# Fewer instructions for the S5 tables, the norms and the reciprocal roots of a two-layer hybrid kernel, and a start that scales one block

## The chip, the cores and the metric

One NeuronCore of one Trainium2 chip runs the whole program. The metric is the time of one execution in device microseconds (us), as the median of several runs; lower is better.

## The reference

Two layers work on 1024 latent and 256 context tokens of width 1024. In each layer the tokens are normalized and modulated, multiplied by an input matrix, sent through four mixers of width 256 (a gated delta rule, S5, SSD, attention), multiplied by an output matrix, normalized and modulated again, and sent through a feed-forward net of width 4096.

```python
def _rms(x, g):
    y = xf * lax.rsqrt(jnp.mean(jnp.square(xf), axis=-1, keepdims=True) + EPS)
def _modulate(h, g, shift, scale):
    return _rms(h, g) * (1.0 + scale) + shift
def s5_mixer(...):
    lam_bar = jnp.exp(lam * jnp.exp(log_step)[..., None])
    b_bar = ((lam_bar - 1.0) / lam)[..., None] * lax.complex(b_re, b_im)
```

The shift and scale come from `cond @ w_mod + b_mod`. S5 is a linear recurrence with complex rates `lam_bar`: 2 directions, 16 groups, 64 states, 16 channels per group.

## The kernel before, in words

**Blocks.** Tokens lie in three blocks: 0 (256 context tokens), 1 and 2 (512 latent tokens each). They are handled in the order 2, 0, 1. Every large product is made of three single-pass products, high by high, high by low and low by high, so each weight and each activation is split into `w_hi`, `w_lo`, `a_hi`, `a_lo`. ACT casts `w_hi`, POOL or DVE subtracts to get `w_lo`; `norm` makes `a_hi` on ACT and `a_lo` on POOL or DVE.

**Streams.** The program is written as generators ("streams"). `Streams.run` always steps the one whose virtual time is least; a step of work adds its cost, divided by the stream's number in `SHARE`, to that time. This sets the order in which instructions are handed over and, with it, their precedence. It is not the final order in an engine: the trace shows small steps of a later S5 setup between steps of an earlier product, so a scheduler fills each engine with what it takes to be ready. On the chip each engine then runs its own queue in order.

**Start** (`main`). `hT` is loaded in three DMAs. The stream "tables" runs `s5_tables(0)`. Beside it `main` spawns `norm_scale` for all three blocks (squares on ACT, a sum tree on DVE, a column of ones on PE, `rsqrt` on DVE, a transpose on PE to spread the root over partitions, `n_acc`) and `mod_pe`, which loads 16 blocks of `w_mod` in four DMAs and computes shift and scale (`md`, `gs`) in four groups on PE. When all are done `norm_next` spawns, block after block, `norm` (`n_x` = h times the root on DVE, then `a_hi`, then `a_lo`), and `w_in1` multiplies by the first part of the input matrix; its first six cells take two weight blocks over blocks 2, 0, 1 in turn.

**S5 tables.** `s5_tables` goes through 2 directions x 2 halves. `s5_setup` loads rates, steps and B, C of 8 groups, and computes the exponential of the step (`exp_acc`, 15 DVE instructions), phases (`s5_reduce`, 5 DVE instructions), sines and cosines (`s5_trig`), 17 complex powers per group (nine for E1 and eight, the same in the other order, for Wo), and the scaled B. Then four calls of `s5_products` each make for two groups `E1` (`5_t_hh`), `ow` (in the tile `5_t_k`), two PE products and two transposes of them, and the two factors `co`, `si`; all goes into a tile `5_fc`, which is stored to DRAM. Every one of these tiles has one buffer. For layer 1 the same stream runs beside the feed-forward net of layer 0 (`extra`), after layer 1's modulation.

**What waits for the tables.** The stream `beside` (gates, gated delta rule, and S5 if the main stream has not taken it) starts when the tables and the norms of the layer are done. `main` goes on with `w_in1`, `w_in2`, SSD, attention, S5, the output matrix, the feed-forward net.

**Reciprocal root.** `rsqrt` starts from a bit trick and makes four Newton steps of four DVE instructions each. It is called for every norm and in the mixers.

Of the kernel before, what the change touches and what calls it, by code (L numbers as in the profile page):

```python
# [36 lines left out]
S5_TB = (("pre", (8, 17)), ("pim", (8, 17)), ("rho", (8,)), ("tsn", (2, 8, 16)), ("tcs", (2, 8, 16)),  # L37
# [21 lines left out]
def const_table():  # L59
    p = np.arange(128)  # L60
    i = np.arange(128)
    c = {}
    c["ident"] = (p[:, None] == i[None]).astype(np.float32)
    c["triU"] = (p[:, None] <= i[None]).astype(np.float32)
    c["triL"] = (p[:, None] >= i[None]).astype(np.float32)
    c["ones"] = np.ones((128, 128), np.float32)
    sel = np.zeros((128, 16), np.float32)
    for k in range(2):
        for pr in range(2):
            for d in range(2):  # L70
# [20 lines left out]
    ex = np.zeros((2, 17), np.float32)  # L91
    ex[0, :9], ex[1, :9] = np.arange(9), 8 - np.arange(9)
    ex[0, 9:], ex[1, 9:] = 7 - np.arange(8), np.arange(8)
    c["ex"] = np.tile(ex.reshape(1, 34), (128, 1))
# [19 lines left out]
class Engine:  # L114
# [14 lines left out]
    def cost(self, op, aps):  # L129
# [4 lines left out]
        if self.name == "tensor":  # L134
# [12 lines left out]
SHARE = {"start": 1.4006, "norm": 7.9949, "mod": 0.7917, "tables": 3.0591, "conv": 0.1388, "ffn": 5.4917,  # L147
# [3 lines left out]
         "ssd_1": 0.8561, "s5_1": 3.3729, "chain": 1.0205, "heads": 0.4024, "scan": 1.0954, "factors": 2.0471}  # L151
# [58 lines left out]
class Core:  # L210
# [57 lines left out]
    def rsqrt(self, pool, out, x, eps, scale, post=1.0):  # L268
# [10 lines left out]
        for k in range(4):  # L279
            nc.vector.tensor_tensor(u, y, y, op=OP.mult)  # L280
            nc.vector.tensor_tensor(u, u, a, op=OP.mult)
            nc.vector.tensor_scalar(u, u, -0.5, 1.5, op0=OP.mult, op1=OP.add)
            o = out if (k == 3 and post == 1.0) else y
            nc.vector.tensor_tensor(o, y, u, op=OP.mult)
# [920 lines left out]
    def s5_tables(self, l, bk, side="left"):  # L1205

        with self.pool("s5w", side) as ws:
            for d in range(2):
                for q in range(2):
                    tb = s5_views(self.t(ws, [128, TBW], F32, "5_tb"), S5_TB)  # L1210
                    yield from self.s5_setup(l, d, q, tb, ws)
                    for n in range(4):
                        fc = self.t(ws, [128, FCW], F32, "5_fc")
                        yield from self.s5_products(l, ws, tb, d, slice(2 * n, 2 * n + 2), s5_views(fc, S5_FC), 4 * q + n, bk)
                        self.nc.sync.dma_start(self.s5d[l][:, 4 * q + n, d], fc)

    def s5_products(self, l, ws, tb, d, x, fc, n, bk):
# [3 lines left out]
        pre, pim, bb, cc, sb2 = [tb[k] for k in ("pre", "pim", "bb", "cc", "sb2")]  # L1221
        E1 = self.t(ws, [128, 2, 9, 16], F32, "5_t_hh")
# [31 lines left out]
        for dst, p0, p1, op in ((fc["co"], (ca, cb), (sa, sb), OP.subtract), (fc["si"], (sa, cb), (ca, sb), OP.add)):  # L1254
# [10 lines left out]
            yield  # L1265

# [54 lines left out]
    def s5_setup(self, l, d, q, tb, ws):  # L1321
        nc, A, c = self.nc, self.A, self.c
        NG = 8
        g0 = 16 * d + 8 * q
        gs = slice(g0, g0 + 8)
        self.mark("5_setup")
        prm = self.t(ws, [128, 3, NG], F32, "5_prm", bufs=1)
        nc.sync.dma_start(prm[:, 0:2], A["s5_a"][l][:, :, gs])
        src = A["s5_ls"][l]
        nc.sync.dma_start(prm[:, 2], bass.AP(tensor=src.tensor, offset=src.offset + g0, ap=[[0, 128], [1, NG]]))  # L1330
# [12 lines left out]
        ex = bc(c["ex"][:, 17 * d:17 * d + 17], 1, NG)
# [4 lines left out]
        mag = self.t(ws, [128, NG, 17], F32, "5_t_b", bufs=1)  # L1348
        nc.gpsimd.tensor_tensor(mag, ex, bc(xd, 2, 17), op=OP.mult)
# [5 lines left out]
        rho = tb["rho"]  # L1355
        nc.vector.tensor_scalar(rho, xd, 8.0, None, op0=OP.mult)
        self.exp_acc(ws, rho, rho, "5_ea")

        ph = self.t(ws, [128, 2, NG], F32, "5_ph", bufs=1)
        t8 = self.t(ws, [128, NG], F32, "5_t8", bufs=1)  # L1360
        nc.vector.tensor_scalar(t8, thr, 8.0, None, op0=OP.mult)
        self.s5_reduce(ws, ph[:, 0], t8, None, "5_q")
        nc.vector.tensor_scalar(t8, ph[:, 0], 16.0, None, op0=OP.mult)
        self.s5_reduce(ws, ph[:, 1], t8, None, "5_q")
        yield
# [3 lines left out]
                                ph.rearrange("p a n -> p (a n)"), bc(c["i16"], 1, 2 * NG), "5_t")  # L1369
# [4 lines left out]
        den = self.t(ws, [128, NG], F32, "5_den", bufs=1)  # L1374
# [9 lines left out]
        nc.vector.tensor_tensor(den, are, are, op=OP.mult)  # L1384
        nc.vector.tensor_tensor(w1, aim, aim, op=OP.mult)
        nc.vector.tensor_tensor(den, den, w1, op=OP.add)
        nc.vector.reciprocal(den, den)
# [245 lines left out]
    def norm(self, wk, h, l, i, cs, hi, lo, rb):  # L1633
# [189 lines left out]
    def main(self, out):  # L1823
# [61 lines left out]
        with self.pool("ms") as pm:  # L1885
# [5 lines left out]
            yield [self.norm_scale(pn, h[i], "g", i, rb) for i in blocks] + [self.mod_pe(0, range(16), 4, 4, pm, ("mm", "mm"))]  # L1891
# [9 lines left out]
        for i in blocks:  # L1901
            norm_next(i, 0, 0, rb[i])
# [217 lines left out]
```

## Time and profile before

| what | value |
|---|---|
| median of 3 runs | 4328.35 us (4321.64 to 4334.05) |
| profiled execution, its own time | 4310.99 us |
| its span | 4309.2 us |
| mean granted TensorE clock | 0.931 |
| PE, DVE, ACT, POOL busy | 3817.7, 2716.2, 1259.1, 1455.5 us |

The profiled execution is 17.4 us below the median of the runs. Busy times are unions over an engine's instructions. A DVE instruction that waits for something inside its execution counts as busy. TensorE's clock is given as a share of full speed.

### The profile page before, as it was taken

To read this page: it belongs to the slowest core of one execution; us is meant where nothing else is said; L and a number is where in the kernel's file an instruction comes from. 1 tells how busy PE (TensorE), PEld (TensorE's weight loads), DVE (VectorE), ACT (ScalarE), POOL (GpSimd) and SP (SyncE) were. 2 spreads that over 40 slices of the span, in tenths; PEclk is the share of its full clock that TensorE was granted. 3 is DMA by queue.
4 is the path that set the end of the run, shared out by engine and by line. 5 is a ranking of instruction groups with operands and counts; after the bars stand their busy time and mean duration, and the time that the engine had idled before them with its cause. 6 is when DMAs were issued, how large, how long until landed. Compare 5 with 4: busy or idle time off the path is not lost.

```text
span 4309.2 us, 61386 instructions
## 1 busy us (share of the span) xinstructions
PE 3817.7 (89%) x23280; PEld 3058.1 (71%) x23280; DVE 2716.2 (63%) x6419; ACT 1259.1 (29%) x2015; POOL 1455.5 (34%) x1664
## 2 busy tenths in 40 slices
PE   5789897789978899999999798997959988999999
PEld 2567776667656688887788677775846676888887
DVE  7966567775644799997775645567765536444443
ACT  3324434333312411121222343244322323222121
POOL 3532533454451211133332224435435433222121
PEclk7899998789999999999999899998969999999999
DMA  5347520100345033311111243342041231111111
GB/s 184 125 159 221 194 98 32 45 2 5 74 123 176 30 98 98 103 60 55 50 62 62 81 136 100 106 144 76 14 106 52 58 135 32 57 40 59 40 59 59
DMA packets 170872, 367.29 MB, mean 85 GB/s; under 512 B 46160, under 2 KB 88400, under 8 KB 166864
## 3 DMA queue, kind: packets, MB, share of 16 engines
q1 hardware_dynamic: 170576, 363.37, 26.2%
q8 instruction: 183, 3.00, 0.3%
q14 instruction: 113, 0.93, 0.1%
HBM read 277.42 MB, written 85.89 MB: 84 GB/s over the span
## 4 chain that ended last, share of the span: by engine, by line
PE 46%; DVE 15%; POOL 3%; DMA 2%; ACT 2%; issue 2%; SPq 0%; DVEq 0%; ACTq 0%; POOLq 0%
PE mm L125 38%; PE m L125 3%; DVE mod_acc L125 3%; PE g L125 2%; PE c L125 2%; DVE h L125 2%; DVE n_x L125 1%; PE x L125 1%; DVE s_ca L125 1%; POOL a_lo L125 1%; POOL g_pr L125 1%; DVE g_scr L125 1%; DVE rsq_u L125 1%; SPq L125 0%; DVE f_r L125 0%
## 5 line engine op out<-in xcount | busy, mean ns | idle before, releaser
L125 PE MATMUL mm<-a_hi,w_hi 128*128 128x512 f32 (+1 forms) x2576 | 978.2, 381 | 45.5 <-ACT st L125 28.6
L125 PE MATMUL mm<-a_lo,w_hi 128*128 128x512 f32 (+1 forms) x2576 | 971.4, 378 | 38.0 <-POOL a_lo L125 18.5
L125 PE MATMUL mm<-a_hi,w_lo 128*128 128x512 f32 (+1 forms) x2576 | 965.8, 375 | 2.4 <-DVE w_lo L125 2.4
L125 POOL TENSOR_TENSOR w_lo<-w_raw,w_hi 128x1024 fp32r<-128x1024 f32 x189 | 465.0, 2469 | 1270.9 <-ACT w_hi L125 1268.9
L125 DVE SCALAR_TENSOR_TENSOR h<-mm,md,h 128x512 f32<-128x512 f32 (+1 forms) x680 | 467.4, 693 | 250.7 <-PE mm L125 246.9
L125 PEld LDWEIGHTS mm<-a_hi,w_hi 128*128 128x128 f32 x2576 | 499.1, 194 | 141.9 <-ACT st L125 32.6
L125 PEld LDWEIGHTS mm<-a_lo,w_hi 128*128 128x128 f32 x2576 | 500.4, 194 | 131.0 <-POOL a_lo L125 30.5
L125 PEld LDWEIGHTS mm<-a_hi,w_lo 128*128 128x128 f32 x2576 | 499.3, 194 | 83.9 <-DVE w_lo L125 2.9
L125 PE MATMUL mm<-f_rh,w_hi 128*128 128x512 f32 (+1 forms) x1280 | 478.3, 374 | 27.8 <-DVE f_r L125 13.7
L125 PE MATMUL mm<-f_rl,w_hi 128*128 128x512 f32 (+1 forms) x1280 | 473.6, 370 | 0.0
L125 PE MATMUL mm<-f_rh,w_lo 128*128 128x512 f32 (+1 forms) x1280 | 473.1, 370 | 0.0
L125 ACT CAST w_hi<-w_raw 128x1024 fp32r<-128x1024 f32 x234 | 242.2, 1048 | 735.5 <-PE mm L125 600.5
L125 DVE SCALAR_TENSOR_TENSOR f_r<-mm,f_r 128x512 f32<-128x512 f32 (+1 forms) x160 | 101.5, 634 | 360.1 <-ACT f_rh L125 359.4
L125 PEld LDWEIGHTS mm<-f_rh,w_hi 128*128 128x128 f32 x1280 | 243.7, 190 | 72.0 <-DVE h L125 16.5
L125 PEld LDWEIGHTS mm<-f_rh,w_lo 128*128 128x128 f32 x1280 | 243.1, 190 | 40.5
L125 PEld LDWEIGHTS mm<-f_rl,w_hi 128*128 128x128 f32 x1280 | 243.5, 190 | 39.1
L125 ACT ACTIVATE f_r<-mm 128x512 f32<-128x512 f32 (+1 forms) x160 | 88.1, 551 | 547.7 <-PE mm L125 474.0
L125 DVE SCALAR_TENSOR_TENSOR mod_acc<-mod_w,cond,mod_acc 128x128 f32<-128x128 f32 x672 | 240.4, 404 | 1.4
L125 POOL TENSOR_TENSOR m_sum<-m_sum,m_p 128x512 f32<-128x512 f32 x128 | 164.1, 1282 | 124.0 <-ACT m_p L125 117.9
L125 DVE SCALAR_TENSOR_TENSOR s_ca<-s_cx,s_prm,s_ca 128x255 f32<-128x255 f32 (+2 forms) x240 | 148.7, 644 | 24.4 <-ACT s_ca L125 22.1
L125 POOL TENSOR_TENSOR a_lo<-n_x,a_hi 128x512 fp32r<-128x512 f32 (+1 forms) x66 | 77.8, 1188 | 154.4 <-DVE n_x L125 139.5
L125 DVE TENSOR_TENSOR f_rl<-f_r,f_rh 128x512 fp32r<-128x512 f32 (+1 forms) x160 | 116.1, 726 | 2.0
(493 smaller groups left out, 6629.0 us busy)
## 6 DMA issues: line engine op xcount, KB each, us to landing
w_raw<-in_w_ff SPq DMA_DIRECT2D x128, 512.0 KB, 3.6
w_raw<-in_w_in SPq DMA_DIRECT2D x90, 512.0 KB, 3.9
mod_w<-in_w_mod SPq DMA_DIRECT2D x80, 512.0 KB, 3.7
pd<-st SPq DMA_DIRECT2D x80, 257.0 KB, 2.3
s5d<-5_fc SPq DMA_DIRECT2D x32, 577.0 KB, 2.8
5_fc<-s5d SPq DMA_DIRECT2D x16, 1154.0 KB, 6.3
g_cx<-pd SPq DMA_DIRECT2D x18, 643.0 KB, 4.9
h<-in_hT SPq DMA_DIRECT2D x4, 2048.0 KB, 9.9
```

What stands on the lines that cost most here:

```text
L125: return f(*args, **kw)
```

## The change

1. `s5_small` does the one-number-per-group work (step, rate, phases, `rho`, the reciprocal of |lambda|^2) for all 32 groups at once, once per layer. `s5_setup` takes slices of it.
2. Nine powers per group instead of 17; Wo reads the same nine in reverse.
3. In `s5_products` the PE part, its copies and the E1 and rho copies go behind the `co`/`si` part; `ow` has a tile of its own, `5_t_o`; the rho copy moves from DVE to ACT.
4. `rsqrt` makes three Newton steps of three instructions instead of four of four.
5. `norm` multiplies h by scale and root in one instruction, `n_x` has three buffers, and the low part is one DVE instruction for odd k, ACT and POOL for even k.
6. At the start only `norm_scale` of block 2 runs beside the modulation; blocks 0 and 1 are scaled by their norm streams.
7. Seven numbers in `SHARE` differ.

```diff
-SHARE = {"start": 1.4006, "norm": 7.9949, "mod": 0.7917, "tables": 3.0591, ..., "ffn": 5.4917,
+SHARE = {"start": 2.8429, "norm": 7.0304, "mod": 0.7934, "tables": 2.7961, ..., "ffn": 6.1066,
-... "mla_1": 1.3799, ... "s5_1": 3.3729, ... "scan": 1.0954
+... "mla_1": 1.4932, ... "s5_1": 5.5532, ... "scan": 1.078
...
-        for k in range(4):
-            nc.vector.tensor_tensor(u, y, y, op=OP.mult)
+        for k in range(3):
+            nc.vector.scalar_tensor_tensor(u, y, -0.5, y, op0=OP.mult, op1=OP.mult)
             nc.vector.tensor_tensor(u, u, a, op=OP.mult)
-            nc.vector.tensor_scalar(u, u, -0.5, 1.5, op0=OP.mult, op1=OP.add)
-            nc.vector.tensor_tensor(o, y, u, op=OP.mult)
+            nc.vector.scalar_tensor_tensor(o, u, 1.5, y, op0=OP.add, op1=OP.mult)
...
     def s5_tables(self, l, bk, side="left"):
+            sm = yield from self.s5_small(l, ws)
...
     def s5_products(...):
         E1 = ...
-        nc.scalar.copy(fc["E1"], E1[:, :, 1 - d:9 - d])
-        ow = self.t(ws, [128, 2, 8, 16], F32, "5_t_k")
+        ow = self.t(ws, [128, 2, 8, 16], F32, "5_t_o")
-        nc.vector.tensor_copy(fc["rho"], tb["rho"][:, x])
-        (PE products of E1, transposes of ow, K and Wo copies, store of K)
         (co and si)
+        (PE products of E1, transposes of ow)
+        nc.scalar.copy(fc["E1"], E1[:, :, 1 - d:9 - d])
+        nc.scalar.copy(fc["rho"], tb["rho"][:, x])
+        (K and Wo copies, store of K)
...
     def s5_setup(...):
-        (loads of prm, exp_acc, xd, th, thr, rho, ph, den, 8 groups wide)
+        (slices of s5_small's tiles; one copy phc)
-        mag = self.t(ws, [128, NG, 17], F32, "5_t_b", bufs=1)
+        mag = self.t(ws, [128, NG, 9], F32, "5_t_b", bufs=1)
...
     def norm(...):
-            x = self.t(wk, [128, 512], F32, "n_x", bufs=2)
-            nc.vector.tensor_tensor(x[:, :w], h[:, k], rb[:, :w], op=OP.mult)
-            nc.scalar.activation(hi[:, k], x[:, :w], AF.Identity, bias=sh, scale=gs)
+            x = self.t(wk, [128, 512], F32, "n_x", bufs=3)
+            nc.vector.scalar_tensor_tensor(x[:, :w], h[:, k], gs, rb[:, :w], op0=OP.mult, op1=OP.mult)
+            nc.scalar.activation(hi[:, k], x[:, :w], AF.Identity, bias=sh)
             if k % 2:
-                nc.scalar.activation(x[:, :w], x[:, :w], AF.Identity, bias=sh, scale=gs)
+                nc.vector.scalar_tensor_tensor(lo[:, k], x[:, :w], sh, hi[:, k].bitcast(F32), op0=OP.add, op1=OP.subtract)
             else:
-                nc.vector.tensor_scalar(x[:, :w], x[:, :w], gs, sh, op0=OP.mult, op1=OP.add)
-            (nc.vector if k % 4 == 3 else nc.gpsimd).tensor_tensor(lo[:, k], x[:, :w], hi[:, k].bitcast(F32), op=OP.subtract)
+                nc.scalar.activation(x[:, :w], x[:, :w], AF.Identity, bias=sh)
+                nc.gpsimd.tensor_tensor(lo[:, k], x[:, :w], hi[:, k].bitcast(F32), op=OP.subtract)
...
-            yield [self.norm_scale(pn, h[i], "g", i, rb) for i in blocks] + [self.mod_pe(0, range(16), 4, 4, pm, ("mm", "mm"))]
+            yield [self.norm_scale(pn, h[2], "g", 2, rb), self.mod_pe(0, range(16), 4, 4, pm, ("mm", "mm"))]
...
-            norm_next(i, 0, 0, rb[i])
+            norm_next(i, 0, 0, rb.get(i))
```

## Rows read from the trace of the kernel before

**Rows 1.** By stretch: us, busy (count) of PE, PEld, DVE, ACT, POOL, PEclk, DMA share, GB/s

```profile
0.00:66.00 66.00, 25.90 (x114) 10.59 (x114) 43.07 (x214) 17.79 (x25) 14.47 (x26) 0.82 0.68 247
66.00:146.00 80.00, 53.39 (x173) 34.92 (x173) 72.58 (x189) 34.29 (x59) 46.73 (x52) 0.74 0.21 77
146.00:282.00 136.00, 105.25 (x502) 78.56 (x503) 110.54 (x335) 30.46 (x70) 65.63 (x105) 0.91 0.37 133
282.00:480.00 198.00, 191.36 (x1524) 152.91 (x1523) 103.61 (x209) 88.84 (x148) 56.77 (x74) 0.97 0.73 234
...
1866.00:2316.00 450.00, 427.76 (x2201) 356.98 (x2201) 334.97 (x860) 96.80 (x180) 151.82 (x157) 0.97 0.18 59
...
2960.00:3440.00 480.00, 397.74 (x3108) 296.74 (x3108) 310.47 (x799) 145.15 (x265) 226.94 (x324) 0.86 0.21 59
...
20.00:40.00 20.00, 8.30 (x42) 2.64 (x42) 18.62 (x109) 8.81 (x11) 1.62 (x3) 0.91 1.03 416
```

**Rows 2.** Timeline of DVE and POOL: start us, us, instruction, idle before; start and end of tables

```profile
66.50 0.69 DVE L125 TENSOR_TENSOR n_x<-h,n_acc 128x512 f32<-128x512 f32 x1
...
68.21 0.16 DVE L125 TENSOR_TENSOR md<-mm,bm 128x8 f32<-128x8 f32 x1
...
281.79 0.97 POOL L125 TENSOR_TENSOR 5_t_r<-5_tb 128x320 f32<-128x320 f32 x1 [2.52 <-DVE 5_fc L125]
```

**Rows 3.** Who PE waited for, 60 to 160 us: us in total, times, longest

```profile
PE mm L125 <- POOL a_lo L125: 10.1, 7, 3.2
...
PE g L125 <- DVE n_rr L125: 5.1, 1, 5.1
```

**Rows 4.** Who PE waited for, 160 to 300 us

```profile
PE g L125 <- DVE 5_t_hh L125: 19.4, 5, 8.9
```

**Rows 5.** DVE groups by shape, 0 to 282 us: count, busy us, mean ns, idle before

```profile
L125 DVE SCALAR_TENSOR_TENSOR 5_ea_p<-5_ea_p,5_ea_r 128x8 f32<-128x8 f32 x48 | 11.5, 240 | 0.3
...
L125 DVE SCALAR_TENSOR_TENSOR 5_t_r<-5_t_k,5_t_r 128x136 f32<-128x136 f32 x16 | 4.7, 293 | 0.1
...
L125 DVE SCALAR_TENSOR_TENSOR 5_t_r<-5_t_k,5_t_r 128x256 f32<-128x256 f32 x8 | 3.3, 417 | 0.1
...
L125 DVE COPY 5_fc<-5_tb 128x2 f32<-128x2 f32 x16 | 3.1, 192 | 1.8 <-DMA s5d<-5_fc 1.8
...
L125 DVE TENSOR_SCALAR 5_ea_r<-5_prm 128x8 f32<-128x8 f32 x4 | 0.6, 150 | 0.0
```

**Rows 6.** Norms, whole run: ns min/median/max, first and last start

```profile
L125 DVE TENSOR_TENSOR n_x<-h,n_acc x88: 410/680/2879, 66.5 to 3620.9; 128x512 f32<-128x512 f32 x64, 128x256 f32<-128x256 f32 x24
...
L125 POOL TENSOR_TENSOR a_lo<-n_x,a_hi x66: 724/1276/2601, 70.8 to 3622.5; 128x512 fp32r<-128x512 f32 x48, 128x256 fp32r<-128x256 f32 x18
L125 DVE TENSOR_SCALAR n_x<-n_x,gs,md x44: 400/541/1968, 70.2 to 3621.9; 128x512 f32<-128x512 f32 x32, 128x256 f32<-128x256 f32 x12
```

**Rows 7.** DVE instructions with and without a number per partition: ns min/median/max

```profile
L125 DVE SCALAR_TENSOR_TENSOR h<-mm,md,h x680: 467/746/752, 1330.4 to 4299.9; 128x512 f32<-128x512 f32 x136, 128x256 f32<-128x256 f32 x34
...
L125 DVE SCALAR_TENSOR_TENSOR f_r<-mm,f_r x160: 404/691/693, 1454.4 to 4279.4; 128x512 f32<-128x512 f32 x128, 128x256 f32<-128x256 f32 x32
```

**Rows 8.** Timeline: a POOL subtraction and the DVE step of a root beside it

```profile
63.40 2.38 POOL L125 TENSOR_TENSOR w_lo<-w_raw,w_hi 128x1024 fp32r<-128x1024 f32 x1 [1.09 <-ACT w_hi L125]
...
63.48 2.32 DVE L125 TENSOR_SCALAR rsq_u<-rsq_u 128x4 f32<-128x4 f32 x1
```

**Rows 9.** Steps of all roots, whole run: ns min/median/max

```profile
L125 DVE TENSOR_TENSOR rsq_u<-rsq_u,rsq_a x108: 142/174/1126, 32.6 to 3604.7; 128x4 f32<-128x4 f32 x32, 128x40 f32<-128x40 f32 x16, 128x20 f32<-128x20 f32 x16, 128x65 f32<-128x65 f32 x16
```

**Rows 10.** Who PE, then DVE waited for, 1865 to 2320 us (tables of layer 1)

```profile
PE mm L125 <- DVE f_r L125: 13.7, 6, 6.8
...
DVE 5_t_k L125 <- PE g L125: 23.8, 13, 3.3
```

**Rows 11.** Who PE waited for, 2400 to 2510 us (norms between the layers)

```profile
PE g L125 <- DVE n_acc L125: 22.9, 4, 17.7
PE g L125 <- DVE n_rr L125: 5.1, 2, 4.6
```

More of the change, by code (lines that the diff above doesn't have):

```diff
@@ L90, in const_table @@
     c["lev"] = np.stack(ms, 1).reshape(128, 256)
[L91 to L94, printed above, removed]
+    ex = np.stack([np.arange(9), 8 - np.arange(9)]).astype(np.float32)
+    c["ex"] = np.tile(ex.reshape(1, 18), (128, 1))
     c["i16"] = np.tile(np.arange(16, dtype=np.float32)[None], (128, 1))
@@ L146 @@
 SIDE = 0.263
-SHARE = {"start": 1.4006, "norm": 7.9949, "mod": 0.7917, "tables": 3.0591, "conv": 0.1388, "ffn": 5.4917,
+SHARE = {"start": 2.8429, "norm": 7.0304, "mod": 0.7934, "tables": 2.7961, "conv": 0.1388, "ffn": 6.1066,
          "w1_0": 0.9376, "w2_0": 1.3776, "prep0_0": 0.1806, "solve0_0": 0.4513, "prep1_0": 0.4642,
          "solve1_0": 0.2102, "mla_0": 0.9476, "ssd_0": 0.8009, "s5_0": 1.3121, "w1_1": 0.7053, "w2_1": 0.9426,
[1 row of a table removed]
-         "ssd_1": 0.8561, "s5_1": 3.3729, "chain": 1.0205, "heads": 0.4024, "scan": 1.0954, "factors": 2.0471}
[1 row of a table added]
+         "ssd_1": 0.8561, "s5_1": 5.5532, "chain": 1.0205, "heads": 0.4024, "scan": 1.078, "factors": 2.0471}
 class Engines:
@@ L278, in rsqrt @@
         u = self.t(pool, sh, F32, "rsq_u")
-        for k in range(4):
-            nc.vector.tensor_tensor(u, y, y, op=OP.mult)
+        for k in range(3):
+            nc.vector.scalar_tensor_tensor(u, y, -0.5, y, op0=OP.mult, op1=OP.mult)
             nc.vector.tensor_tensor(u, u, a, op=OP.mult)
-            nc.vector.tensor_scalar(u, u, -0.5, 1.5, op0=OP.mult, op1=OP.add)
-            o = out if (k == 3 and post == 1.0) else y
-            nc.vector.tensor_tensor(o, y, u, op=OP.mult)
+            o = out if (k == 2 and post == 1.0) else y
+            nc.vector.scalar_tensor_tensor(o, u, 1.5, y, op0=OP.add, op1=OP.mult)
         if post != 1.0:
@@ L1210, in s5_tables @@
                     tb = s5_views(self.t(ws, [128, TBW], F32, "5_tb"), S5_TB)
-                    yield from self.s5_setup(l, d, q, tb, ws)
+                    tb["rho"] = sm[5][:, 16 * d + 8 * q:16 * d + 8 * q + 8]
+                    yield from self.s5_setup(l, d, q, tb, ws, sm)
                     for n in range(4):
@@ L1221, in s5_products @@
         pre, pim, bb, cc, sb2 = [tb[k] for k in ("pre", "pim", "bb", "cc", "sb2")]
+        rev = lambda z: z[:, x, 7::-1] if d == 0 else z[:, x, 8:0:-1]
         E1 = self.t(ws, [128, 2, 9, 16], F32, "5_t_hh")
@@ L1265, in s5_products @@
             yield
+        b = self.bank(bk)
+        for g in range(2):
+            self.mm(b[0:16, 128 * g:128 * g + 128], bb[:, 0, x][:, g], E1[:, g, d:8 + d].rearrange("p s c -> p (s c)"))
+            self.tr(b[:, 256 + 128 * g:384 + 128 * g], ow[:, g].rearrange("p s c -> p (s c)"))
+        nc.scalar.copy(fc["E1"], E1[:, :, 1 - d:9 - d])
+        nc.scalar.copy(fc["rho"], tb["rho"][:, x])
+        K = self.t(ws, [16, 2, 8, 16], F32, "5_t_p")
+        K0 = self.t(ws, [16, 2, 16], F32, "5_K0")
+        if d == 1:
+            nc.sync.dma_start(K0, self.s5k[l][:, n, :, 7])
+        nc.scalar.copy(K, b[0:16, 0:256].rearrange("p (g s c) -> p g s c", g=2, s=8))
+        nc.scalar.copy(fc["Wo"], b[:, 256:512].rearrange("p (g x) -> p g x", g=2))
+        if d == 1:
+            nc.vector.tensor_tensor(K[:, :, 7], K[:, :, 7], K0, op=OP.add)
+        nc.sync.dma_start(self.s5k[l][:, n, :, 7 - 7 * d:15 - 7 * d], K)
+        yield
     def s5(self, l, put, bk, side="left", ctx_out=True, bufs=3):
@@ L1319, in s5_weights, with s5_small @@
         return sd, wg
-    def s5_setup(self, l, d, q, tb, ws):
+    def s5_small(self, l, ws):
+        nc, A = self.nc, self.A
+        self.mark("5_small")
+        prm = self.t(ws, [128, 3, 32], F32, "5_prm", bufs=1)
+        nc.sync.dma_start(prm[:, 0:2], A["s5_a"][l])
+        src = A["s5_ls"][l]
+        nc.sync.dma_start(prm[:, 2], bass.AP(tensor=src.tensor, offset=src.offset, ap=[[0, 128], [1, 32]]))
+        are, aim, dl = prm[:, 0], prm[:, 1], prm[:, 2]
+        self.exp_acc(ws, dl, dl, "5_ea")
+        xd, th, thr, rho, t8, den, w1 = [self.t(ws, [128, 32], F32, f"5_{n}", bufs=1)
+                                         for n in ("xd", "th", "thr", "rho", "t8", "den", "w1s")]
+        nc.vector.tensor_tensor(xd, are, dl, op=OP.mult)
+        nc.vector.tensor_tensor(th, aim, dl, op=OP.mult)
+        self.s5_reduce(ws, thr, th, None, "5_q")
+        yield
+        nc.vector.tensor_scalar(rho, xd, 8.0, None, op0=OP.mult)
+        self.exp_acc(ws, rho, rho, "5_ea")
+        yield
+        ph = self.t(ws, [128, 2, 32], F32, "5_ph", bufs=1)
+        nc.vector.tensor_scalar(t8, thr, 8.0, None, op0=OP.mult)
+        self.s5_reduce(ws, ph[:, 0], t8, None, "5_q")
+        nc.vector.tensor_scalar(t8, ph[:, 0], 16.0, None, op0=OP.mult)
+        self.s5_reduce(ws, ph[:, 1], t8, None, "5_q")
+        nc.vector.tensor_tensor(den, are, are, op=OP.mult)
+        nc.vector.tensor_tensor(w1, aim, aim, op=OP.mult)
+        nc.vector.tensor_tensor(den, den, w1, op=OP.add)
+        nc.vector.reciprocal(den, den)
+        yield
+        return are, aim, xd, thr, ph, rho, den
@@ L1322, in s5_setup @@
+    def s5_setup(self, l, d, q, tb, ws, sm):
         nc, A, c = self.nc, self.A, self.c
         NG = 8
-        g0 = 16 * d + 8 * q
-        gs = slice(g0, g0 + 8)
+        gs = slice(16 * d + 8 * q, 16 * d + 8 * q + 8)
         self.mark("5_setup")
[L1327 to L1330, printed above, removed]
@@ L1340, in s5_setup @@
-        self.s5_reduce(ws, thr, th, None, "5_q")
-        yield
-        ex = bc(c["ex"][:, 17 * d:17 * d + 17], 1, NG)
+        are, aim, xd, thr = [z[:, gs] for z in sm[0:4]]
+        ph, den = sm[4][:, :, gs], sm[6][:, gs]
+        ex = bc(c["ex"][:, 9 * d:9 * d + 9], 1, NG)
         pre = tb["pre"]
@@ L1383, in s5_setup @@
         nc.vector.tensor_copy(ni, pim[:, :, m])
[L1384 to L1387, printed above, removed]
         nc.vector.tensor_tensor(w1, nr, are, op=OP.mult)
```

44 lines of the change are left out of this document (7 added, 37 removed), and 2 rows, old and new, of the table SHARE.

## The prediction, made before the changed kernel was run

> **What bounds the kernel now.** I read the busy times by stretch first. After 282 us the PE is busy 191.4 of 198 us [rows 1], so there only PE work counts, and a microsecond gained before it moves everything behind it. Before 282 us it is not: PE is idle 40.1 us of the first 66, 26.6 of the next 80 and 30.8 of the next 136, while DVE is busy 72.6 of 80 and 110.5 of 136 [rows 1]. So the front of the kernel is bound by DVE and by what PE waits for. The timeline says what ends there: the first `n_x` comes at 66.5 us, the last group of the modulation at 68.2, and the tables' last factor at 281.8 [rows 2]; `beside` cannot start earlier than that. The list of waits gives the reasons: PE waits 10.1 us for `a_lo` of POOL, 5.1 us in one piece for a root of `norm_scale` [rows 3], and 19.4 us for `5_t_hh` of the tables [rows 4]. That last one is PE standing in its own queue before an S5 product whose input DVE has not finished. The tables of layer 1 lie beside the feed-forward net, where PE is idle only 450.0 - 427.8 = 22.2 us [rows 1].
>
> **The change, part by part.** First the front of layer 0, where I count DVE time.
>
> *One-number work.* A setup has 54 such instructions (two exponentials of 15, three reductions of 5, nine others), four setups have 216. Their groups, from 48 at 240 ns to 4 at 150 ns [rows 5], add up to 49.7 us. Afterwards there are 54 of them plus four copies, so 158 go. At the mean that is 158 / 216 x 49.7 = 36 us. The other bound: neighbours in the pipeline overlap, and at half of 150 ns each it is 158 x 0.075 = 12 us. I take 24, the middle, since they run partly as a chain and partly between other work. 32 columns for 8 cost 24 columns more: 256 against 136 columns is 417 against 293 ns [rows 5], 1.03 ns a column, so 54 x 0.025 = 1.3 us. Net 23 us. The loads on SP's queue go from 12 to 6, two of the six four times as wide; I cost that at nothing, covered by the other setup's work until it is wanted, and a wait that were not covered would shrink with the count.
>
> *Nine powers.* Per setup 11 instructions of the sines and 15 of the exponential shrink from 136 to 72 columns: 26 x 64 x 1.03 ns = 1.7 us, times four 6.9 us. It can't be a loss; if those instructions are hidden it is 0.
>
> *Rho on ACT.* 16 DVE copies cost 3.1 us and 1.8 us of waiting for the store of the tile [rows 5]. Taken: 4 us. ACT, busy 30.5 of 136 us [rows 1], takes them on.
>
> *Roots.* 19 instructions become 12. A step lasts 0.174 us [rows 9], so a root is 1.2 us shorter, three roots 3.7 us. The trace shows what I need to weigh here: a step over four columns took 2.32 us beside a POOL subtraction of 2.38 us [rows 8]. The removed step reads one tensor; the three that stay read two.
>
> The Trainium skill, page SBUF — State Buffer, section Who interferes with whom, says that a DVE instruction with two SBUF inputs, or one in a two-port mode, and a GpSimd instruction that reads SBUF block each other whole. That speaks against this part, since every step of the new loop has two such inputs: where POOL is at work nothing would be won on roots, and the sum below would be 8 us smaller. The row agrees as to the blocking, but there the blocked step is of the removed kind, so I go by the rows.
>
> *Norm.* Per 512-wide block DVE has now 8 x 0.680 + 4 x 0.541 + 2 x 0.68 = 9.0 us [rows 6], the low parts taken like `n_x`. A number per partition adds about 0.055 us (746 against 691 ns) [rows 7], so the new one has 12 x 0.735 = 8.8 us. No difference. ACT keeps 12 instructions a block. POOL loses 2 of 6 `a_lo`, 2.6 us a block. I cost it at nothing, because DVE is the busier engine; uncovered it is worth up to 6 us.
>
> *PE part moved.* In a product PE now comes after `co`/`si`, so it should find E1 and `ow` done: the 19.4 us [rows 4] go. What is late next: `5_t_hh` and `5_t_o` are freed only at the end of a product, so the next product's first POOL instruction waits for PE and ACT; `a_lo` and `w_lo` stand behind it on POOL. Today the wait for PE falls on DVE's `5_t_k`, 1.8 us each time beside the feed-forward net [rows 10], as near to the PE instruction as the new one, so I take 0 for the difference. Ends: -16 and +50 us (rival C).
>
> *Start.* `hT` and 16 blocks of `w_mod` are 13.6 MB by their shapes; at the 416 GB/s of [rows 1] they are in after about 37 us. The last group of the modulation stood behind PE's 5.1 us for another block's root [rows 3]. Without two of three scales I estimate the first `n_x` at 50 us, between 40 and 66. But the two scales only move: their DVE work falls between the norms.
>
> Two ways to the front's sum: DVE loses 23 + 7 + 4 + 4 = 38 us. PE loses 16 (start) + 19 (`5_t_hh`) = 35 us of idle, if the middle stretch keeps its 26.6 us. They are two sights of the same gain, not to be added: **36 us**, bounds 12 (one-number work at its low end, nothing else) and 57 (all PE idle behind the first 40 us).
>
> *Elsewhere.* Layer 1's tables lose the same 34 us without the roots, but beside a PE that is idle 22.2 us; DVE's 13.7 us of late `f_r` [rows 10] is the largest part. I take half, **11 us**, bounds 0 and 22. The other 24 roots lose 24 x 1.2 = 29 us of DVE; on the path are some, as the 5.1 us of waiting for `n_rr` between the layers [rows 11] show. I take a quarter, **8 us**, bounds 0 and 29. The numbers in `SHARE` reorder layer 1's mixers, where PE is idle 82 of 480 us [rows 1]: taken 0, bounds a fifth of that idle either way, 16 us.
>
> **Sum:** 36 + 11 + 8 = 55 us. Against the profiled execution's own 4311.0 us that is 4256; it lies 17.4 us below the median of the runs, so I forecast 4328.4 - 55 = **4273 us** for the median.
>
> **Rivals.**
>
> *B, PE starves between the blocks.* Scaling now stands in the chain norm 2, scale 0, norm 0, scale 1, norm 1. Between the layers the same chain stands alone, and PE waits 22.9 + 5.1 = 28.0 us in three blocks [rows 11], 9.3 each. Two blocks moved give back 19 us: gain 36, 4292 us. For it: `w_in1` has only two cells per block to cover with. Against it: squares and sums of block 0 need nothing of block 2, so they can be slipped in earlier.
>
> *C, slower.* The wait at the head of each product. POOL waits for PE's S5 product, that one stands behind a cell of `w_in1` or the net, and the cell waits for a `w_lo` behind the waiting POOL instruction. At the longest wait seen, 3.3 us [rows 10], 32 products cost 106 us: 4328 + 106 - 55 = 4379 us. It decides from 55 / 32 = 1.7 us per product on. Against it: the scheduler has `co`/`si` and the next setup to put between.
>
> *D, PE keeps its clock.* The granted clock is 0.74 and 0.91 between 66 and 282 us [rows 1], a mixture of the levels 1.2 and 2.4 GHz, behind stretches where PE paused. If PE runs there without pauses at the upper level, 53.4 us of work become 39.5 and 105.3 become 95.8: 23 us more, 4250 us.
>
> *E, nothing measurable.* DVE's gain is real, but the small instructions ran in gaps, and the order that the new numbers in `SHARE` give takes the rest back: about 4325 us.
>
> **How the numbers follow.** Forecast 0.60, B 0.17, D 0.12, C 0.07, E 0.04. A measurement of this kernel tells 0.3%, 13 us, from no change. Faster by more: the forecast, D and nearly all of B, 0.87; within: E and B's worst end, 0.05; slower: C and an unlucky order, 0.08. The range: at the low end 57 in front, 22 beside the net, 8 and the order's 16 give 103, short of which I stop at 100, 4228 us. At the high end the front's 12 and nothing else give 4316; B with the order's loss of 16 gives 4308. I put 4318, which leaves out C, E and a little.
>
> **What would show it.** Right: the first `n_x` near 50 us, the tables' last factor near 245, one-number groups with a quarter of the count, PE's wait for `5_t_hh` gone, and the stretch behind as dense as before. B shows as PE waiting for `n_acc` and `n_rr` between 50 and 140 us. C shows as POOL waiting for PE `g` or ACT `5_fc` on `5_t_hh` or `5_t_o`, over 1.7 us each time, with PE waiting for `w_lo`. D shows as granted clock over 0.95 from 66 to 245. If the tables end near 245 and the total has not moved, the path of the front is not theirs. If they end near 280, DVE's small instructions were no burden.

## The result, and the profile after

| | before | after |
|---|---|---|
| median of the runs on one chip | 4325.23 us (4 runs) | 4257.60 us (4 runs, 4244.92 to 4265.14) |
| ratio, 95% interval | | 0.9838 [0.9809, 0.9867] |
| profiled execution, its span | 4310.99, 4309.2 us | 4244.92, 4243.1 us |

The kernel became 68 us faster by the medians and 66 us by the spans of the two profiled executions. Each of these two is the fastest of its own kernel's runs, so they may be set beside each other; single runs of one kernel differ by 20 us and more (before: 4310.99 to 4334.05).

After, from the page: the span, and busy time, share and count of each engine.

```profile
span 4243.1 us, 60800 instructions
...
PE 3807.5 (90%) x23280; PEld 3063.5 (72%) x23280; DVE 2624.0 (62%) x5860; ACT 1246.1 (29%) x2046; POOL 1429.5 (34%) x1642
```

DVE lost 92 us of busy time and 559 instructions, while PE has the same 23280 as before. Of the 66 us of span, PE standing less gives 56 (491.5 us idle before, 435.6 after) and its own busy time the other 10. To find where, I took the start of the same PE instruction in both traces at the borders of stages. From the timeline of PE before: the first product of layer 0's feed-forward net, its 761st (of 768), and the 1639th product of the input and output matrices (counted by their `a_hi,w_lo` instructions), which lies in layer 1's first cells (start us, us, instruction).

```profile
1466.00 0.39 PE L125 MATMUL mm<-f_rh,w_lo 128*128 128x512 f32 x1
...
2428.97 0.39 PE L125 MATMUL mm<-f_rh,w_lo 128*128 128x512 f32 x1
...
2577.53 0.39 PE L125 MATMUL mm<-a_hi,w_lo 128*128 128x512 f32 x1
```

The same three after:

```profile
1444.57 0.40 PE L123 MATMUL mm<-f_rh,w_lo 128*128 128x512 f32 x1
...
2380.92 0.39 PE L123 MATMUL mm<-f_rh,w_lo 128*128 128x512 f32 x1
...
2509.56 0.39 PE L123 MATMUL mm<-a_hi,w_lo 128*128 128x512 f32 x1
```

The first stage gave 21 us, the net 963.0 - 936.3 = 27, the stretch between the layers 148.6 - 128.6 = 20, and the rest of layer 1 nothing. I had put 36 of 55 us into the front. With the end of the input matrix (505th product) as one more border, every kernel of this study stands in one table. All columns are in us and come from one profiled execution each.

| kernel | front | mixers | net | between | rest |
|---|---|---|---|---|---|
| before | 590.9 | 875.1 | 963.0 | 148.6 | 1721.9 |
| after | 570.4 | 874.2 | 936.3 | 128.6 | 1724.2 |
| before + tables | 571.7 | 878.3 | 957.8 | 146.7 | 1725.4 |
| before + root | 590.2 | 879.4 | 963.5 | 138.7 | 1729.5 |
| before + norm, root | 596.3 | 880.9 | 957.3 | 128.6 | 1720.4 |
| before + tables, norm, root | 570.3 | 877.9 | 950.7 | 131.7 | 1723.6 |
| after, old norm and root | 579.5 | 873.5 | 943.9 | 146.5 | 1722.2 |
| after, old norm | 575.6 | 877.8 | 937.9 | 139.4 | 1723.4 |
| after, old root | 573.2 | 890.9 | 935.6 | 136.4 | 1724.4 |
| after, old `SHARE` | 588.8 | 880.4 | 948.5 | 128.1 | 1730.0 |
| after, old start | 573.7 | 881.4 | 936.8 | 128.6 | 1720.5 |
| after, `s5_small` in every setup | 586.2 | 877.6 | 961.6 | 131.5 | 1725.0 |
| after, PE part early | 573.5 | 881.1 | 936.4 | 129.8 | 1723.5 |
| after, old start, PE part early | 572.0 | 874.9 | 931.0 | 129.6 | 1721.4 |

The columns "net" and "between" fall into a few levels that follow the edits. "Mixers" and "rest" scatter by 17 and 10 us without any pattern, and that scatter is in every single run's total. "Rest" ends with the start of the last product of layer 1's net. The profiled execution is the slowest of its kernel's in experiments 1, 2, 4, 5, 7, 8, 9 and 10 and the fastest before, after and in 3, 6 and 12, so the sum of a row is not a median.

That "rest" gained nothing hides two movements. The windows of this stage, before and after (us, then busy us and count of PE, PEld, DVE, ACT, POOL, the granted clock, DMA share, GB/s):

```profile
2577.53:4299.46 1721.93, 1567.66 (x9464) 1253.83 (x9463) 909.09 (x1843) 494.89 (x757) 585.95 (x626) 0.94 0.23 70
...
2509.56:4233.79 1724.23, 1581.43 (x9464) 1265.99 (x9463) 890.46 (x1766) 487.96 (x754) 577.08 (x622) 0.94 0.22 70
```

PE's idle time falls from 154.3 to 142.8 us, and its busy time for the same number of products rises by 13.8. This follows the root: the four kernels with the old one have 151 to 154 us idle here and 1568 to 1574 busy, the ten with the new one 139 to 146 and 1579 to 1588. Why PE is busy longer there, no run shows.

**The front.** Timeline after, PE, ACT and DVE (start us, us, instruction, idle before):

```profile
49.32 3.64 PE L123 MATMUL mm<-mod_w,condp 128*32 128x512 f32 x16
...
56.86 0.40 ACT L123 COPY 5_fc<-5_t_hh 128x256 f32<-128x256 f32 x1 [8.45 <-DVE 5_t_hh L123]
...
56.98 0.58 PE L123 MATMUL g<-5_t_hh,5_tb 128*16 128x128 f32 x2 [4.02 <-DVE 5_t_hh L123]
...
58.12 0.58 ACT L123 COPY mod_s<-mm 128x512 f32<-128x512 f32 x1
...
58.75 1.87 PE L123 MATMUL mm<-ctab,mod_s 128*128 128x2 f32 x8
...
62.27 0.16 DVE L123 SCALAR_TENSOR_TENSOR gs<-md,g 128x16 f32<-128x16 f32 x1
...
62.69 0.74 DVE L123 SCALAR_TENSOR_TENSOR n_x<-h,gs,n_acc 128x512 f32<-128x512 f32 x1
...
191.40 0.59 PE L123 MATMUL g<-5_t_hh,5_tb 128*16 128x128 f32 x2 [8.78 <-DVE 5_t_hh L123]
...
260.22 0.56 DVE L123 TENSOR_TENSOR 5_fc<-5_t_r,5_t_k 128x64 f32<-128x64 f32 x2 [0.63 <-POOL 5_t_r L123]
```

The first `n_x` comes at 62.7 us, 4 us earlier than before [rows 2], and not near 50. The other blocks' roots no longer stand before the last modulation group, but an S5 product now does: PE waits 4.02 us for its `5_t_hh`, and the group's product follows behind at 58.75. ACT's queue stands behind the same tile: it is idle 8.45 us before it copies `5_t_hh`, and the copy `mod_s`, which the group's product reads, comes behind that and ends at 58.70. `gs` follows at 62.27, and the new `n_x` reads it. The tables' last factor ends at 260.8, 23 us earlier than before; there it ended at 283.4, behind the POOL step of [rows 2].

Groups of DVE instructions after, 0 to 261 us by shape (count, busy us, mean ns, idle before):

```profile
L123 DVE SCALAR_TENSOR_TENSOR 5_t_r<-5_t_k,5_t_r 128x72 f32<-128x72 f32 x16 | 3.7, 232 | 0.4
...
L123 DVE SCALAR_TENSOR_TENSOR 5_ea_p<-5_ea_p,5_ea_r 128x32 f32<-128x32 f32 x12 | 2.4, 196 | 0.0
```

Against [rows 5] these are 12 for 48 instructions, and 232 for 293 ns. Windows after, columns as in [rows 1]:

```profile
0.00:261.00 261.00, 173.95 (x772) 121.44 (x773) 200.72 (x537) 79.69 (x167) 119.56 (x175) 0.84 0.43 155
...
1836.00:2296.00 460.00, 448.87 (x2314) 375.99 (x2313) 332.83 (x767) 101.02 (x201) 155.68 (x158) 0.99 0.18 60
```

Beside layer 1's tables PE is idle 11.1 us, half of the 22.2 before [rows 1], in a window 10 us longer. Who PE waited for after, in 50 to 160, 160 to 300, 1865 to 2320 and 2320 to 2510 us (us in total, times, longest):

```profile
PE g L123 <- DVE 5_t_hh L123: 15.4, 3, 8.2
...
PE g L123 <- DVE n_acc L123: 5.8, 3, 2.6
PE g L123 <- DVE n_rr L123: 2.5, 1, 2.5
...
PE g L123 <- DVE 5_t_hh L123: 18.9, 3, 8.8
...
PE mm L123 <- DVE h L123: 5.4, 2, 5.1
PE mm L123 <- DVE f_r L123: 5.0, 3, 3.6
...
PE g L123 <- DVE n_acc L123: 13.4, 3, 7.2
PE g L123 <- DVE n_rr L123: 3.2, 1, 3.2
```

The wait for `5_t_hh` is still there, 18.9 against 19.4 us [rows 4]; `f_r` fell from 13.7 [rows 10] to 5.0, and `n_acc` with `n_rr` between the layers from 28.0 [rows 11] to 16.6.

**Between the layers.** Timeline of DVE before: from the root of one block to the square sum of the next.

```profile
2418.48 0.16 DVE L125 TENSOR_SCALAR rsq_a<-g 128x4 f32<-128x4 f32 x1
...
2429.58 0.16 DVE L125 TENSOR_TENSOR n_rr<-rsq_y,rsq_u 128x4 f32<-128x4 f32 x1
...
2431.17 1.29 DVE L125 TENSOR_TENSOR n_x<-h,n_acc 128x512 f32<-128x512 f32 x2 [0.34 <-ACT n_acc L125]
...
2434.98 4.49 DVE L125 TENSOR_TENSOR n_x<-h,n_acc 128x512 f32<-128x512 f32 x2 [0.75 <-POOL a_lo L125]
...
2450.11 1.73 DVE L125 TENSOR_TENSOR n_x<-h,n_acc 128x512 f32<-128x512 f32 x1 [1.38 <-POOL a_lo L125]
2451.88 0.29 DVE L125 TENSOR_TENSOR n_acc<-n_sq 128x128 f32<-128x128 f32 x1
```

The same after:

```profile
2369.94 0.16 DVE L123 TENSOR_SCALAR rsq_a<-g 128x4 f32<-128x4 f32 x1
...
2376.77 0.15 DVE L123 SCALAR_TENSOR_TENSOR n_rr<-rsq_u,rsq_y 128x4 f32<-128x4 f32 x1
...
2378.75 2.08 DVE L123 SCALAR_TENSOR_TENSOR n_x<-h,gs,n_acc 128x512 f32<-128x512 f32 x3
...
2382.40 3.50 DVE L123 SCALAR_TENSOR_TENSOR n_x<-h,gs,n_acc 128x512 f32<-128x512 f32 x3
...
2387.81 4.50 DVE L123 SCALAR_TENSOR_TENSOR n_x<-h,gs,n_acc 128x512 f32<-128x512 f32 x2
...
2392.89 0.27 DVE L123 TENSOR_TENSOR n_acc<-n_sq 128x128 f32<-128x128 f32 x1
```

The root takes 6.8 us for 11.1, because each step has about 0.4 us of other DVE work behind it. From the first `n_x` to the next block's `n_acc` it is 14.1 us for 20.7: before, DVE waits four times, 4.7 us in all, for POOL's `a_lo` to free one of two `n_x` buffers; after, these waits are gone. PE's column of ones for the next block needs that `n_acc`, and PE's queue stands behind it: 17.7 us at the longest before [rows 11], 7.2 after.

### The profile page after: what moved, and what is told of

It reads as the page before. It is cut to its first block, busy times and chain, and to the rows that moved or that the text cites. A ratio compares the mean times of both kernels' runs of the same rounds, so it can differ in the third digit from the quotient of the medians.

```text
span 4243.1 us, 60800 instructions
## 1 busy us (share of the span) xinstructions
PE 3807.5 (90%) x23280; PEld 3063.5 (72%) x23280; DVE 2624.0 (62%) x5860; ACT 1246.1 (29%) x2046; POOL 1429.5 (34%) x1642
## 4 chain that ended last, share of the span: by engine, by line
PE 64%; DVE 14%; POOL 4%; DMA 3%; issue 3%; ACT 2%; SPq 1%; ACTq 0%; POOLq 0%; DVEq 0%
PE mm L123 47%; PE m L123 6%; PE c L123 4%; PE g L123 3%; PE x L123 3%; DVE mod_acc L123 1%; DVE s_ca L123 1%; DVE g_scr L123 1%; DVE n_x L123 1%; POOL g_pr L123 1%; DMA s_cx<-pd 1%; SPq L123 1%; DVE h L123 1%; DMA g_cx<-pd 1%; POOL w_lo L123 1%
## 5 line engine op out<-in xcount | busy, mean ns | idle before, releaser
L123 PE MATMUL mm<-f_rh,w_hi 128*128 128x512 f32 (+1 forms) x1280 | 478.9, 374 | 16.2 <-DVE h L123 11.1
L123 PE MATMUL x<-m_p,m_va 128*64 128x256 f32 x656 | 108.1, 398 | 0.6 <-DVE m_rc L123 0.6
```

The lines of the kernel that those rows point to most:

```text
L123: return f(*args, **kw)
```

## The experiments

Every kernel below computes the whole reference. Each result is the median and the ratio to the kernel before on the same chip, with its 95% interval. Where a result is set against the median after, the two may come from different chips; the kernel before had medians of 4325.23 to 4327.73 us on all of them.

**1. The old norm loop in the kernel after.**

```diff
-            x = self.t(wk, [128, 512], F32, "n_x", bufs=3)
-            nc.vector.scalar_tensor_tensor(x[:, :w], h[:, k], gs, rb[:, :w], op0=OP.mult, op1=OP.mult)
+            x = self.t(wk, [128, 512], F32, "n_x", bufs=2)
+            nc.vector.tensor_tensor(x[:, :w], h[:, k], rb[:, :w], op=OP.mult)
...
+            (nc.vector if k % 4 == 3 else nc.gpsimd).tensor_tensor(lo[:, k], x[:, :w], hi[:, k].bitcast(F32), op=OP.subtract)
```

> The changed kernel with the old loop of norm (two buffers, the scale in the ACT instruction, low parts on POOL and DVE). By the prediction's step on the norm (DVE 9.0 against 8.8 us a block) nothing is lost: about 4258 us, within 6. If instead the new loop is what made the stretches around the norms shorter (22 to 25 us in three of them behind the front), they come back: 4270 to 4282 us, with PE waiting longer for a_lo or a_hi beside the output matrix of layer 0 and between the layers.

Measured: 4264.84 us, 0.9855 [0.9835, 0.9874]; "between" 139.4 us, 11 longer than after. By the medians it costs 7 us, within the intervals.

**2. The old root in the kernel after.**

```diff
-        for k in range(3):
-            nc.vector.scalar_tensor_tensor(u, y, -0.5, y, op0=OP.mult, op1=OP.mult)
+        for k in range(4):
+            nc.vector.tensor_tensor(u, y, y, op=OP.mult)
```

> The changed kernel with four Newton steps of four instructions. By the prediction's step (1.2 us a root, a quarter on the path) 8 us are lost: about 4266 us. If the roots are what shortened the norm stretches, 20 us or more: 4278 us. If the scheduler hides them, 4258 us.

Measured: 4264.55 us, 0.9847 [0.9822, 0.9872]; "between" 136.4 us, 8 longer than after. Each part alone is at the edge of what the totals can tell, but the stretch shows it.

**3. Both old (after, old norm and old root).** The edits of experiments 1 and 2 together.

> The changed kernel with both the old norm loop and the old root; each alone cost 7 us. If the two add up: 4272 us. If each can stand in for the other, as the 35 us of the two alone on the kernel before say: about 4290 us, and PE's longest wait for n_acc between the layers is back at some 17 us from 7.

Measured: 4290.60 us, 0.9908 [0.9886, 0.9929], 33 us more than after; "between" 146.5 us, near the level of the kernel before.

**4. The new root alone, in the kernel before.**

> The kernel before with the new root alone. By the theory that either change of the norm path suffices: 4325 - 28 = 4297 us, with the wait for n_acc between the layers at 13 us instead of 23. By adding up single effects: 4318 us. By the prediction's 12 us: 4313 us.

Measured: 4310.02 us, 0.9956 [0.9941, 0.9971], 18 us less than before; "between" 138.7 us.

**5. New norm and new root, in the kernel before.**

> The kernel before with the new norm loop and the new root alone. By the prediction: roots 8 and 4 in front, norm nothing: 4327 - 12 = 4315 us. By the first experiments (7 each): 4313 us. If they only help where SHARE has moved the norms onto the path: 4327 us within 6.

Measured: 4290.67 us, 0.9911 [0.9895, 0.9928], 35 us less; "between" 128.6 us, exactly as after.

The five and the two original kernels make a square for the stretch between the layers: 146.5 to 148.6 us with neither, 138.7 and 139.4 with the root, 136.4 with the norm, 128.6 with both (128.1 to 131.7 in the eight kernels of the table that have both). The root is worth 7 to 10 us there, the norm 10 to 11, and they add up. The waits of PE in that stretch say the same. With neither (experiment 3):

```profile
PE g L123 <- DVE n_acc L123: 23.8, 4, 17.7
PE g L123 <- DVE n_rr L123: 5.1, 2, 4.6
```

With the new root alone (experiment 1, where the norm is old):

```profile
PE g L123 <- DVE n_acc L123: 17.6, 4, 13.0
PE g L123 <- DVE n_rr L123: 3.4, 2, 3.2
```

With the new norm alone (experiment 2):

```profile
PE g L123 <- DVE n_acc L123: 17.6, 4, 13.9
PE g L123 <- DVE n_rr L123: 5.1, 2, 4.6
```

28.9, 21.0 and 22.7 us, and 16.6 with both. In the net they do not add up: one of the two is enough. With neither (experiment 3), PE waits there once for a root:

```profile
PE g L123 <- DVE n_rr L123: 5.7, 1, 5.7
```

In experiments 1 and 2 this wait is gone, and the net is 6 and 8 us shorter than in 3. Before, and still in experiment 6, it is 4.9 us, and in experiment 5, where it is gone, the net is 5.7 us shorter. So 33 us for both and 7 us for each alone need not contradict each other. Against experiment 3 the stages of the kernel after place 35 us: 18 between, 8 in the net and 9 in the front. In the kernel before (experiment 5) they place 20 and 6, and its front is 5 us longer. So what norm and root do in the front depends on the rest of the arrangement and is not explained here.

**6. The changed tables alone, in the kernel before.** `s5_small`, nine powers, rho on ACT, PE part late; old norm, root, start and `SHARE`.

> The kernel before with the changed tables alone (one-number work at once, nine powers, PE part last, rho on ACT); norm, root, start and SHARE are the old ones. By the prediction, front 32 and net 11 without roots and start: 4327 - 43 = 4284 us. By what the stretches and the first experiments show (roots and norm 7 each, SHARE 21, start -8 of a gain of 68): 68 - 27 = 41, 4286 us. By the theory that the order of the streams makes most of it: under 25, over 4302 us.

Measured: 4297.83 us, 0.9932 [0.9916, 0.9949], 28 us less than before, between what was expected of the parts and what the order of the streams alone would leave. The front is 19 us shorter, nearly all of the 21 that the whole change gains there; the net 5.

**7. `s5_small` once per setup in the kernel after**, which brings back 162 small DVE instructions a layer, though over 32 columns.

```diff
-            sm = yield from self.s5_small(l, ws)
             for d in range(2):
                 for q in range(2):
+                    sm = yield from self.s5_small(l, ws)
```

> The changed kernel with s5_small called once per setup instead of once per layer: 162 more small DVE instructions in each layer's tables, none removed. By the prediction (23 us of DVE in front, the path of the front) the first tables end some 20 us later and the total is 4270 to 4285 us. By the rival that the one-number work runs in gaps and was no burden: 4258 us within 5, tables' end within 8 us of the changed kernel's 261.

Measured: 4283.89 us, 0.9899 [0.9880, 0.9918], 26 us more than after; the tables of layer 0 end at 270.0 us. The front is 16 us longer, the net 25. Who PE waited for in it, 1865 to 2320 us:

```profile
PE mm L123 <- DVE f_r L123: 16.3, 5, 6.0
PE mm L123 <- DVE h L123: 13.0, 4, 5.1
```

29.3 us against 10.4 after. So it is the number of the small instructions that costs, in the front and beside the net; DVE's waits for the loads that come back with them are 0.5 us. The sizes are less sure: 16 and 25 come from the slowest of this kernel's runs and are together more than the 26 us of the medians. Nine powers and rho on ACT were not tried by themselves.

**8. The PE part of a product back between `ow` and `co`/`si`, in the kernel after.**

```diff
+        b = self.bank(bk)
+        for g in range(2):
+            self.mm(b[0:16, 128 * g:128 * g + 128], bb[:, 0, x][:, g], E1[:, g, d:8 + d].rearrange("p s c -> p (s c)"))
...
         for dst, p0, p1, op in ((fc["co"], (ca, cb), (sa, sb), OP.subtract), (fc["si"], (sa, cb), (ca, sb), OP.add)):
```

> The changed kernel with the PE part of a product (products, transposes, copies) back between ow and co/si; the tile of its own for ow stays. By the prediction's step (PE's wait for 5_t_hh goes when PE comes last) PE should wait longer for 5_t_hh and the total rise by up to 16 us: 4265 to 4274 us. The changed kernel still shows 15.4 and 18.9 us of that wait between 50 and 300 us, so by the rival the place changes nothing: 4258 us within 5, the same wait of about 34 us.

Measured: 4250.18 us, 0.9820 [0.9804, 0.9836], not distinguishable from after. PE's waits in 50 to 160 and 160 to 300 us:

```profile
PE g L123 <- DVE 5_t_hh L123: 15.4, 3, 8.2
...
PE g L123 <- DVE 5_t_hh L123: 19.1, 3, 8.8
```

They are the same as after. The place of the PE part doesn't set this wait. The timeline after shows what may: the wait of 8.78 us that ends at 191.40 is for the first product of a setup, and in it DVE works through that setup's sines (128x256 steps of 0.42 us) almost without a pause. No run here moved that.

**9. The old `SHARE` in the kernel after.**

```diff
-SHARE = {"start": 2.8429, "norm": 7.0304, "mod": 0.7934, "tables": 2.7961, "conv": 0.1388, "ffn": 6.1066,
+SHARE = {"start": 1.4006, "norm": 7.9949, "mod": 0.7917, "tables": 3.0591, "conv": 0.1388, "ffn": 5.4917,
```

> The changed kernel with the old seven numbers in SHARE, no other difference. By the theory that work taken away gives the gain, the numbers count little: 4258 us within 10. By the rival that the order makes the gain in the norm stretches and beside the net, about 25 us come back: 4283 us, most of it between 1330 and 2500 us; the front keeps its 20.

Measured: 4278.56 us, 0.9887 [0.9864, 0.9911], 21 us more than after; the net is 12 us longer, the front 18.

**10. The old start in the kernel after:** `norm_scale` of all blocks beside the modulation.

```diff
-            yield [self.norm_scale(pn, h[2], "g", 2, rb), self.mod_pe(0, range(16), 4, 4, pm, ("mm", "mm"))]
+            yield [self.norm_scale(pn, h[i], "g", i, rb) for i in blocks] + [self.mod_pe(0, range(16), 4, 4, pm, ("mm", "mm"))]
```

> The changed kernel with norm_scale of all three blocks beside the modulation again, as before, with the new numbers. If the start's 16 us of the prediction are real, the first n_x comes some 15 us later than in the changed kernel and the total rises by 5 to 16 us. If the two scales that were moved are paid for between the norms (rival B), the total stays at 4258 us within 5, or falls.

Measured: 4249.69 us, 0.9815 [0.9791, 0.9838]: 8 us less than after, with intervals that overlap. The first `n_x` comes 5 us later (67.9) and the tables end 22 us later (282.8), but the front as a whole is 573.7 for 570.4 us. So the end of the tables is not what ends the front: here it lies as late as before (283.4) and the front is short, in experiment 12 too (283.5 and 572.0), while in experiment 9 the tables end at 255.2 and the front is 588.8.

**11. Tables, norm and root in the kernel before; old start, old `SHARE`.**

> The kernel before with the changed tables, norm and root, but the old start and the old SHARE. If the gains of the two halves (28 and 35) add up, 4325 - 62 = 4263 us, and the start and the numbers in SHARE are together worth 5. If the numbers in SHARE are worth the 21 us that the changed kernel loses without them and the new start costs 8: 4257 + 21 - 8 = 4270 us.

Measured: 4265.33 us, 0.9857 [0.9835, 0.9879], 62 us less than before, as much as experiments 5 and 6 together (35 + 28). Experiment 10 differs from it by `SHARE` alone: 16 us by the medians, and 950.7 - 936.8 = 14 us in the net. The windows show how. Busy times in 1630 to 1730 us, the first half of the net, here:

```profile
1630.00:1730.00 100.00, 96.31 (x536) 83.87 (x535) 98.90 (x260) 18.50 (x28) 20.68 (x8) 1.00 0.33 106
```

and in experiment 10:

```profile
1630.00:1730.00 100.00, 99.28 (x550) 86.56 (x548) 94.56 (x248) 18.38 (x28) 20.29 (x8) 1.00 0.31 99
```

With the old numbers DVE is full with layer 1's modulation beside the net (its last `mod_acc` starts at 1836 us; at 1879 with the new ones), and PE waits for DVE. The new ones give the net more and the side streams less, so modulation and tables are spread thinner; the tables' last DVE instruction comes at 2318 for 2243 us, and that costs nothing. Of the 14 us, 7 are PE standing less and 7 PE's busy time. In the front the old numbers do no harm together with the old start (570.3), but with the new one the front is 18 us longer (588.8): those numbers and the start seem to belong together. Which number does it wasn't tried.

**12. Old start and early PE part in the kernel after.**

> The changed kernel with all three scales at the start again and the PE part back in the middle of a product, the two edits that lost nothing when undone (-8 and -7 us). If both are real and apart: 4242 us. If they are the scatter of one order against another: 4250 to 4260 us.

Measured: 4243.61 us, 0.9814 [0.9791, 0.9836], the lowest median of the study, 14 us below after. The intervals overlap, so it is not shown to be faster; it does show that neither move is needed for the gain.

## Why the prediction was right, and where its terms were not

The forecast was 55 us, a median of 4273; 68 came, 4257.60, inside the range. The sum was nearer than its terms, and that is in part luck: the front and layer 1's tables came 21 us short, and the norm loop and `SHARE`, both put at nothing, gave more than that:

| term | predicted, us | by the stages, us | from |
|---|---|---|---|
| front of layer 0 | 36 (12 to 57) | 19 to 21 | experiment 6; after |
| layer 1's tables beside the net | 11 (0 to 22) | 5 | experiment 6 |
| roots elsewhere | 8 (0 to 29) | 7 to 10 between; with the norm loop 6 to 8 in the net | experiments 1 to 5 |
| norm loop | 0 (up to 6) | 10 to 11 between | experiments 1 to 5 |
| `SHARE` | 0 (16 either way) | 14 | experiment 11 against 10 |

- **Front: less DVE work was right, the path was not, and the term was too large.** Of its two sights, "DVE loses 38 us" and "PE loses 35 us of idle", the first came out at two thirds: DVE's busy time up to the end of the tables fell by 26 us (226.6 in 283 us before, 200.7 in 261 after). The second came out at 10 us: in the same windows PE's idle time went from 97 to 87 us. Up to the 505th product it went from 120.4 to 108.9; the other 9 us of the front's gain are PE's busy time. Three steps failed. "The 19.4 us go": they didn't, and in 50 to 160 us the same wait even rose from 4.8 to 15.4, since I took it for a matter of order within a product and experiment 8 shows that it is not. "First `n_x` at 50 us": 62.7, because removing what PE waited for in front of the last modulation group let an S5 product take its place, and PE's and ACT's queues both stood behind its `5_t_hh`. I named no successor for that wait. And the tables' last factor, put near 245 and found at 260.8, was taken for what ends the front; experiments 9, 10 and 12 show that it isn't. Which wait does end it stays open.
- **One-number work**: the count was right and the price about right. 158 fewer instructions were put at 23 us in front; 162 brought back cost 16 there. Beside the net I gave the whole of layer 1's tables 11; the whole change of the tables won 5 there (experiment 6), and bringing the small instructions back cost 25 in one execution (experiment 7). Why the two differ isn't shown.
- **Norm loop, costed at nothing "because DVE is the busier engine"**: this was the wrong step. DVE's own time stayed as predicted (12 x 0.74 us a block), but DVE wasn't short of time; it waited for POOL's `a_lo` to free `n_x`, and with DVE waited the next block's `n_acc` and PE. The 5.1 and 22.9 us in [rows 11] were on record, and I used them only for roots and for rival B. The bound "uncovered up to 6 us" was too low as well, as it took POOL's busy time, 2.6 us a block, and no wait. The three parts of the new loop (one instruction for scale and root, a third buffer, fewer parts on POOL) were tried only together; that the buffer is the reason is read from the timeline, where these waits are 4.7 of the 6.6 us, and isn't shown by a run.
- **Roots**: a step was taken at 0.174 us. In the stretch that counts DVE puts an `h` of 0.48 us between two steps, so seven steps fewer gave 4.3 us a root and not 1.2. That 8 us came out near is luck, by two errors against each other: 1.2 us a root was too low, and a quarter of the roots on the path, at 4.3 us each, would be 26 us, more than any stage shows.

The rule of the Trainium skill (page SBUF — State Buffer, section Who interferes with whom) would have taken 8 us from the sum. Experiment 4 decides against that: the new root alone won 18 us by the median. The rule itself isn't refuted, for in the kernel after POOL stood idle for 16.64 us, and the root between the layers, 2369.94 to 2376.77, lies in that time with nothing to block it:

```profile
2381.61 3.07 POOL L123 TENSOR_TENSOR a_lo<-n_x,a_hi 128x512 fp32r<-128x512 f32 x2 [16.64 <-ACT n_x L123]
```

- **`SHARE`**: I looked for it in layer 1's mixers, where "rest" shows nothing, and it acted in the net. Its size, 14, is near the bound of 16.
- **Rivals.** B, PE starving for the moved scales: 5.8 and 2.5 us of waiting for `n_acc` and `n_rr` in 50 to 160 us are small, and experiment 10 puts its price at 8 us by medians and at nothing by the front; not settled. C fell: POOL does wait for PE's `g` beside the net, 51.9 us in 10 waits after against 79.0 in 9 before, but PE's waits for `w_lo` don't show. D was not seen: the granted clock up to the tables' end is 0.84 before and after. E fell by the result.

## What to carry to other kernels

A loop's price is not the busy time of its busiest engine: look which buffer it waits for, who frees it, and which engine stands in its own queue for what comes behind that loop. Short dependent steps on an in-order engine cost what the scheduler puts between them, not their own duration, so read their spacing in the stretch that matters. The instruction that ends last in a stage need not be what the next stage waits for: look for a run in which it moved and the stage did not. When a wait at the head of a queue is removed, look for the next instruction that can slip in there, and test numbers that steer the order apart from the work, because they belong to one arrangement of it.

## What the runs showed of the hardware

A small DVE instruction with two inputs can last as long as a POOL subtraction beside it, not only one with a single input as in [rows 8]. Timelines after, POOL and DVE:

```profile
179.29 2.43 POOL L123 TENSOR_TENSOR w_lo<-w_raw,w_hi 128x1024 fp32r<-128x1024 f32 x1
...
179.39 2.35 DVE L123 TENSOR_TENSOR 5_wi<-5_w,5_w 128x8 f32<-128x8 f32 x1
...
182.00 0.16 DVE L123 TENSOR_TENSOR 5_wi<-5_wi,5_den 128x8 f32<-128x8 f32 x1
```

Eight columns took 2.35 us, where 0.16 is usual in the same stretch. The Trainium skill, page SBUF — State Buffer, section Who interferes with whom, says that a DVE instruction with two SBUF inputs contends with a GpSimd (POOL) instruction that reads SBUF, and here the row agrees. The new `n_x`, with a number per partition, has a median of 0.746 us against 0.680 of the old one without [rows 6], both mostly over 512 columns.
